# Two more blocks of the residual turned by DMA, and another order of k pairs, in a two-layer trunk kernel

## The chip, the cores and the metric

The kernel runs on one core of one Trainium2 chip. The metric is the device time of one execution in microseconds (us), as the median of several runs. A core has five engines that run side by side, each through its own list of instructions in order: TensorE (PE, matrix products, its weight loads shown as PEld), VectorE (DVE), ScalarE (ACT), GpSimd (POOL) and SyncE (SP), which here issues nearly all DMA transfers. Engines wait for one another through semaphores.

## What is computed

The reference is a decoder trunk of two layers over a residual stream h of 256 rows and 2048 columns, in float32:

```python
for layer in range(DEPTH):                       # DEPTH = 2
    xn = rms_norm(h, norm_mix[layer])
    mix = swa_mlstm_mixer(xn, ...) if layer % 2 == 0 else forgetting_attention_mixer(xn, ...)
    h = h + mix                                  # both mixers end in "@ w_out"
    h = h + swiglu(rms_norm(h, norm_ffn[layer]), w_gate[layer], w_up[layer], w_down[layer])
return rms_norm(h, norm_final)

def swiglu(xn, w_gate, w_up, w_down):            # 2048 -> 5632 -> 2048
    return (silu(xn @ w_gate) * (xn @ w_up)) @ w_down
```

The change lies where a mixer's output projection (`@ w_out`) ends and the gate and up products of the same layer begin.

## The kernel before, in words

Every product is made in three passes: each float32 operand is split into a high part in the fast float32r format and a low part, the remainder, and PE adds high x high, high x low and low x high (lines 192 to 194 and `three`, lines 402 to 404). The activations sit transposed in `xh`/`xl` (after a norm) and `mh`/`ml` (a mixer's heads or the hidden columns), 16 k-tiles of 128. The weights come in chunks of two k-tiles by 512 columns: SP loads a chunk into `raw` (line 105), ACT casts it to `hi` (line 161), DVE subtracts to `lo` (line 162). There are four `raw` buffers (pool `wr`) and six of `hi` and `lo` each (pool `wp`). One chunk feeds 12 matmuls.

`out_proj` (line 386) makes the four blocks n of 512 columns of the mixer's output, two at a time: first 12 of 16 k-tiles of both, then the last four k-tiles of one and of the other. After each block `add_out` (line 300, DVE) adds it to h, and `square_sum` (line 215, ACT) sums its squares for the next norm. Then the block of h has to be transposed into `xh`/`xl`, k-tiles 4n to 4n+3, that is the k pairs 2n and 2n+1. The kernel has two ways:

- `split_scaled` (line 238): PE transposes 128 x 128 pieces into PSUM (line 245), ACT multiplies by the norm's gain to `xh` (line 252), DVE makes `xl` (line 253).
- `split_turned` (line 268): ACT copies the two 16-bit halves of each number into two planes (line 272), SP issues four DMA transposes (line 274); later `join` lets ACT weave the planes together (line 279) and goes on as above from SBUF. It needs two scratch tiles (`scrap`, line 284), which borrow buffers of a later use.

Before the change blocks 0 and 1 are turned by DMA, while the other two blocks are being multiplied; blocks 2 and 3 are turned on PE. `LATER` gives the step of out_proj at which a join is issued; `run_due` (line 172) issues it behind the latest cast of a chunk.

`ffn` (line 473) takes 11 groups of 512 hidden columns, in parts of three, four and four; after each part its down product follows. A group is `pair_group` (line 409): it walks the eight k pairs of `xh` in the order of `ORDER`, for gate and up together. A pair marked 0 is plain: two chunks, 24 matmuls (here called P). A pair marked 1 is taken in seven products in place of eight (here called M): DVE makes four sums and differences of the weights in `t4` (lines 440 to 443), ACT and DVE split them into `ht` and `lt` (lines 294 and 295), and PE makes 21 matmuls against sums of the activations (`sx`), which `sums_of` (line 227) made when the block was split. Four PSUM banks hold the plain sums and four the products; the next group takes them the other way round. `c` and `u2` (lines 466 to 470) put the products together, line 494 adds the plain banks.

The order of the instructions on each engine is laid by the framework's planner from the dependencies; only `run_due` sets a bound by hand. SP's queue holds the loads and the DMA transposes in one order.

Of the kernel before, what the change touches and what calls it, by code (L numbers as in the profile page):

```python
# [7 lines left out]
F32 = mybir.dt.float32  # L8
BF16 = mybir.dt.bfloat16
F32R = mybir.dt.float32r  # L10
# [7 lines left out]
P = 128  # L18
# [3 lines left out]
KT = D // P  # L22
FF = 5632
NB = 512
CK = 2
# [7 lines left out]
OFF_QM, OFF_KM, OFF_VM, OFF_OM = 1536, 2048, 2560, 3584  # L33
CAP = 15.0
FILL = 24
ORDER = ((0, 0), (0, 1), (1, 2), (0, 4), (1, 3), (0, 5), (1, 6), (0, 7))
DOWN = {
    6: ((0, 0), (0, 1), (1, 2), (0, 3), (0, 4), (0, 5)),
    8: ((0, 0), (0, 1), (0, 3), (1, 2), (0, 4), (1, 5), (0, 6), (0, 7)),
}  # L40
MID = 6
MID_DOWN = 5
LATER = (6, 10)
LATER_DOWN = (5, 6)
RAWS = 4
PARTS = (0, 3, 7, 11)
# [2 lines left out]
def mixed_of(order):  # L49
    return [p for w, p in order if w]  # L50
# [5 lines left out]
def trunk(  # L56
# [110 lines left out]
    def new_acc():  # L167
        return [pa.tile([P, NB], F32, tag="acc", name="acc") for _ in range(NT)]

    later = []  # L170
# [6 lines left out]
    def gemm(acc, lhs, w, c0, n, k_from, k_to, k_all, skew=1, step=0):  # L177
        k0 = k_from
        while k0 < k_to:
            last = k_to == k_all and k0 + skew * CK >= k_all  # L180
            chunks = [load_chunk(w, kc, c0, n) for kc in range(k0, k_all if last else k0 + CK, CK)]
            run_due(later, step + k0 // CK)
            order = [(i, t) for i in range(len(chunks) * CK) for t in range(NT)]
            if last:
                order.sort(key=lambda it: it[1])
            for i, t in order:
                k = k0 + i
                hi, lo = (c[:, i % CK, 0:n] for c in chunks[i // CK])
                ah, al = lhs(k)
                ts = slice(t * P, (t + 1) * P)  # L190
                o = acc[t][:, 0:n]
                nc.tensor.matmul(o, ah[:, ts], hi, start=(k == 0), stop=False)  # L192
                nc.tensor.matmul(o, ah[:, ts], lo, start=False, stop=False)  # L193
                nc.tensor.matmul(o, al[:, ts], hi, start=False, stop=(k == k_all - 1))  # L194
            k0 += len(chunks) * CK
# [14 lines left out]
    def square_sum(key, n):  # L210
        if n == 0:
            sums[key] = sm.tile([P, NT, 4], F32, tag="ss", name="ss")
        for t in range(NT):
            junk = sm.tile([P, NB], BF16, tag="junk", name="junk", bufs=1)
            nc.scalar.activation(
                junk, h[:, t, n * NB : (n + 1) * NB], AF.Square, accum_out=sums[key][:, t, n : n + 1]
            )
# [9 lines left out]
    def sums_of(pool, sh, sl, copies, full=None):  # L227
        if full is None:
            full = pool.tile([P, 2, NT, P], F32, tag="tmp", name="full")
            copies(full.rearrange("p i t q -> p i (t q)"))  # L230
        s = pool.tile([P, 4, P], F32, tag="tmp", name="s4")
        nc.vector.tensor_tensor(out=s[:, 0, :], in0=full[:, 0, 1, :], in1=full[:, 1, 1, :], op=ALU.add)
        nc.vector.tensor_tensor(out=s[:, 1, :], in0=s[:, 0, :], in1=full[:, 0, 0, :], op=ALU.subtract)
        nc.vector.tensor_tensor(out=s[:, 2, :], in0=full[:, 0, 0, :], in1=full[:, 0, 1, :], op=ALU.subtract)
        nc.vector.tensor_tensor(out=s[:, 3, :], in0=full[:, 1, 0, :], in1=s[:, 1, :], op=ALU.subtract)
        split_plain(sh, sl, s)

    def split_scaled(idx, n, extra=None, joined=None):
        for half in range(2):
            if joined is None:  # L240
                pt = pm.tile([P, 2, NT, P], F32, tag="pm", name="pt")
                for i in range(2):
                    k = 4 * n + 2 * half + i
                    for t in range(NT):
                        nc.tensor.transpose(pt[:, i, t, :], h[:, t, k * P : (k + 1) * P], ident)  # L245
            else:
                pt = joined[:, 2 * half : 2 * half + 2, :].rearrange("p i (t q) -> p i t q", t=NT)
            for i in range(2):
                k = 4 * n + 2 * half + i
                src = pt[:, i, :, :].rearrange("p t q -> p (t q)")  # L250
                g = gT[:, idx * KT + k : idx * KT + k + 1]
                nc.scalar.mul(xh[:, k, :], src, g)
                nc.vector.scalar_tensor_tensor(
                    out=xl[:, k, :], in0=src, scalar=g, in1=xh[:, k, :].bitcast(F32), op0=ALU.mult, op1=ALU.subtract
                )
            pair = 2 * n + half
            if extra is not None and pair in mixed_of(ORDER):
                sh, sl, pool = extra
                j = mixed_of(ORDER).index(pair)

                def copies(full):
                    for i in range(2):
                        g = gT[:, idx * KT + 2 * pair + i : idx * KT + 2 * pair + i + 1]
                        nc.scalar.mul(full[:, i, :], pt[:, i, :, :].rearrange("p t q -> p (t q)"), g)

                sums_of(pool, sh[:, j, :, :], sl[:, j, :, :], copies)

    def split_turned(idx, n, flat, turned, extra=None):
        planes = flat.bitcast(U16).rearrange("p (b t n) -> p b t n", b=2, t=NT)
        hu = h[:, :, n * NB : (n + 1) * NB].bitcast(U16).rearrange("p t (n b) -> p t n b", b=2)  # L270
        for b in range(2):
            nc.scalar.copy(planes[:, b, :, :], hu[:, :, :, b])
            for t in range(NT):
                nc.sync.dma_start_transpose(turned[:, b, :, t, :], planes[:, b, t, :])

        def join():
            ju = flat.bitcast(U16).rearrange("p (n b) -> p n b", b=2)
            for b in range(2):
                nc.scalar.copy(ju[:, :, b], turned[:, b, :, :, :].rearrange("p k t q -> p (k t q)"))
            split_scaled(idx, n, extra, flat.rearrange("p (k s) -> p k s", k=4))  # L280

        return join

    def scrap(fp, n):
        if n == 0:
            box = fp.tile([P, 4, NB], F32, tag="c", name="box", bufs=1)
            halves = box[:, 0:2, :], box[:, 2:4, :]
        else:
            halves = [fp.tile([P, CK, NB], F32, tag="raw", name="box", bufs=RAWS) for _ in range(2)]
        flat, turned = (a.rearrange("p a n -> p (a n)") for a in halves)  # L290
        return flat, turned.bitcast(U16).rearrange("p (b k t q) -> p b k t q", b=2, t=NT, q=P)
# [92 lines left out]
            split_plain(mh[:, ks, :], ml[:, ks, :], po)  # L384

    def out_proj(w, idx, key, extra):
        last = KT - 4
        for n0 in (0, 2):
            accs = [new_acc() for _ in range(2)]
            for i in range(2):  # L390
                gemm(accs[i], m_of, w, (n0 + i) * NB, NB, 0, last, KT, step=6 * i)
            for i in range(2):
                gemm(accs[i], m_of, w, (n0 + i) * NB, NB, last, KT, KT, step=6)
                add_out(accs[i], n0 + i)
                if n0 == 0:
                    later.append((LATER[i], split_turned(idx, i, *scrap(extra[2], i), extra)))
                else:
                    split_scaled(idx, n0 + i, extra)
                square_sum(key, n0 + i)

    def three(o, ah, al, hi, lo, start, stop):
        nc.tensor.matmul(o, ah, hi, start=start, stop=False)  # L402
# [67 lines left out]
        nc.vector.tensor_tensor(out=c[:, 3, :], in0=prods[1], in1=c[:, 1, :], op=ALU.add)  # L470
        return plain, c

    def ffn(layer, fp, sx, sd, key, idx_next=None, key_next=None, finish=None):
        r = rstd(key)

        def sums_x(pair):
            j = mixed_of(ORDER).index(pair)
            return sx[0][:, j, :, :], sx[1][:, j, :, :]

        for g0, g1 in zip(PARTS, PARTS[1:]):  # L480
            end = g1 == PARTS[-1]
            nk = 4 * (g1 - g0)
            order = DOWN[nk // 2]
            todo = []
            for g in range(g0, g1):
                par = (g1 - 1 - g) % 2
                plain, c = pair_group(
                    fp, par, x_of, sums_x, [(w_gate[layer], g * NB), (w_up[layer], g * NB)], ORDER, todo
                )
                todo = []  # L490
# [54 lines left out]
                todo = [(MID if g < g1 - 1 else MID_DOWN, join)]  # L545
# [20 lines left out]
            for n0 in (0, 2):  # L566
# [9 lines left out]
                todo = []  # L576
# [10 lines left out]
    def close_layer(layer, w_out, idx, key, **rest):  # L587
        with tc.tile_pool(name=f"fp{layer}", bufs=2) as fp:
            nx = len(mixed_of(ORDER))
            nd = max(len(mixed_of(o)) for o in DOWN.values())  # L590
            sx = [fp.tile([P, nx, 4, P], F32R, name=f"sx{i}", bufs=1) for i in range(2)]
            sd = [fp.tile([P, nd, 4, P], F32R, name=f"sd{i}", bufs=1) for i in range(2)]
            out_proj(w_out, idx, key, (*sx, fp))
            ffn(layer, fp, sx, sd, key, **rest)


    acc0 = new_acc()
# [417 lines left out]
```

## Time and profile before

| what | value |
|---|---|
| median of 3 runs | 2132.01 us (2131.75 to 2132.25) |
| the profiled execution | 2131.7 us |
| its span, first to last instruction | 2130.0 us |
| PE busy | 2113.6 us, 9732 instructions |
| DVE busy | 1666.1 us |
| ACT busy | 1256.1 us |
| DMA transposes of h by out_proj (line 274, with the four of one block at the end of the first layer) | 20 |
| PE transposes of h (line 245) | 88 |
| mean granted TensorE clock | 0.998 |

The first layer's out_proj ends and its gate and up products begin near 348 us, the second layer's near 1428 us. Times of the trace count from the span's start. A busy time is a sum over instructions of one engine. Matmuls overlap in PE's pipeline, so the time that one costs is the distance from its start to the next one's, not its own span.

### The profile page before, as it was taken

To read this page: it belongs to the slowest core of one execution; us is meant where nothing else is said; L and a number is where in the kernel's file an instruction comes from. 1 tells how busy PE (TensorE), PEld (TensorE's weight loads), DVE (VectorE), ACT (ScalarE), POOL (GpSimd) and SP (SyncE) were. 2 spreads that over 40 slices of the span, in tenths; PEclk is the share of its full clock that TensorE was granted. 3 is DMA by queue.
4 is the path that set the end of the run, shared out by engine and by line. 5 is a ranking of instruction groups with operands and counts; after the bars stand their busy time and mean duration, and the time that the engine had idled before them with its cause. 6 is when DMAs were issued, how large, how long until landed. Compare 5 with 4: busy or idle time off the path is not lost.

```text
span 2130.0 us, 26773 instructions
## 1 busy us (share of the span) xinstructions
PE 2113.6 (99%) x9732; PEld 1755.0 (82%) x9732; DVE 1666.1 (78%) x2116; ACT 1256.1 (59%) x1584; POOL 39.6 (2%) x61
## 2 busy tenths in 40 slices
PE   8999999999999999999999999999999999999998
PEld 7888888888888888888888888888888888888886
DVE  6665558998899988998755554579998998889984
ACT  6565457765567646666645544576654667556753
POOL 2010000000000000000010000000000000000000
PEclk9999999999999999999999999999999999999999
DMA  8444547665667666766575564675756666656763
GB/s 268 149 150 148 169 150 265 217 208 197 198 207 225 211 207 193 235 206 198 163 235 168 168 178 142 195 247 187 238 188 208 207 208 206 228 189 208 228 200 125
DMA packets 267941, 421.47 MB, mean 198 GB/s; under 512 B 67136, under 2 KB 75424, under 8 KB 267552
## 3 DMA queue, kind: packets, MB, share of 16 engines
q1 hardware_dynamic: 267136, 416.02, 61.5%
q0 software_dynamic: 624, 3.72, 0.5%
q8 instruction: 76, 1.25, 0.2%
q14 instruction: 57, 0.47, 0.1%
q10 hardware_dynamic: 48, 0.02, 0.0%
HBM read 404.48 MB, written 2.11 MB: 191 GB/s over the span
## 4 chain that ended last, share of the span: by engine, by line
PE 98%; ACT 1%; issue 0%; DMA 0%; DVE 0%; DVEq 0%; POOLq 0%; POOL 0%; ACTq 0%
PE acc L402 17%; PE acc L403 17%; PE acc L404 17%; PE acc L192 10%; PE acc L193 10%; PE acc L194 10%; PE prod L402 4%; PE prod L404 4%; PE prod L403 4%; PE p L323 1%; PE ptm L306 1%; PE po L374 1%; PE pt L245 0%; PE pp L366 0%; PE p L316 0%
## 5 line engine op out<-in xcount | busy, mean ns | idle before, releaser
L161 ACT CAST hi<-raw 128x1024 fp32r<-128x1024 f32 (+1 forms) x692 | 705.1, 1033 | 667.3 <-PE acc L404 314.4
L162 DVE TENSOR_TENSOR lo<-raw,hi 128x1024 fp32r<-128x1024 f32 (+1 forms) x692 | 821.5, 1200 | 314.7 <-ACT hi L161 312.9
L403 PE MATMUL acc<-lo,xh 128*128 128x512 f32 x946 | 368.1, 389 | 0.0
L404 PE MATMUL acc<-hi,xl 128*128 128x512 f32 x946 | 367.2, 389 | 0.0
L402 PE MATMUL acc<-hi,xh 128*128 128x512 f32 x946 | 366.5, 389 | 0.0
L192 PE MATMUL acc<-hi,xh 128*128 128x512 f32 (+3 forms) x736 | 276.7, 377 | 0.8 <-ACT hi L161 0.8
L194 PE MATMUL acc<-hi,xl 128*128 128x512 f32 (+3 forms) x736 | 276.8, 377 | 0.0
L193 PE MATMUL acc<-lo,xh 128*128 128x512 f32 (+3 forms) x736 | 276.3, 375 | 0.0
L404 PEld LDWEIGHTS acc<-hi,xl 128*128 128x128 f32 x946 | 177.6, 188 | 36.9
L403 PEld LDWEIGHTS acc<-lo,xh 128*128 128x128 f32 x946 | 177.6, 188 | 36.7
L402 PEld LDWEIGHTS acc<-hi,xh 128*128 128x128 f32 x946 | 177.6, 188 | 36.6
L295 DVE TENSOR_TENSOR lt<-t,ht 128x1024 fp32r<-128x1024 f32 x168 | 199.7, 1217 | 3.6 <-ACT ht L294 3.6
L403 PE MATMUL acc<-lo,mh 128*128 128x512 f32 x514 | 200.2, 389 | 0.0
L402 PE MATMUL acc<-hi,mh 128*128 128x512 f32 x514 | 200.0, 389 | 0.0
L404 PE MATMUL acc<-hi,ml 128*128 128x512 f32 x514 | 198.5, 389 | 0.0
L294 ACT CAST ht<-t 128x1024 fp32r<-128x1024 f32 x168 | 174.8, 1052 | 20.8 <-PE acc L404 12.8
L192 PEld LDWEIGHTS acc<-hi,xh 128*128 128x128 f32 x736 | 139.0, 189 | 25.0 <-ACT hi L161 1.2
L194 PEld LDWEIGHTS acc<-hi,xl 128*128 128x128 f32 x736 | 139.1, 189 | 24.4 <-issue 0.8
L193 PEld LDWEIGHTS acc<-lo,xh 128*128 128x128 f32 x736 | 139.2, 189 | 24.0 <-issue 0.7
L192 PE MATMUL acc<-hi,mh 128*128 128x512 f32 x320 | 125.2, 391 | 1.2 <-ACT mh L294 1.2
L193 PE MATMUL acc<-lo,mh 128*128 128x512 f32 x320 | 125.3, 392 | 0.0
L194 PE MATMUL acc<-hi,ml 128*128 128x512 f32 x320 | 123.9, 390 | 0.0
(311 smaller groups left out, 2779.4 us busy)
## 6 DMA issues: line engine op xcount, KB each, us to landing
raw<-in_w_gate_dram SPq DMA_DIRECT2D x176, 512.0 KB, 4.3
raw<-in_w_up_dram SPq DMA_DIRECT2D x176, 512.0 KB, 4.6
raw<-in_w_down_dram SPq DMA_DIRECT2D x176, 512.0 KB, 4.6
raw<-in_w_in_odd_dram SPq DMA_DIRECT2D x88, 512.0 KB, 3.8
raw<-in_w_in_even_dram SPq DMA_DIRECT2D x64, 512.0 KB, 4.0
raw<-in_w_out_even_dram SPq DMA_DIRECT2D x32, 512.0 KB, 3.6
raw<-in_w_out_odd_dram SPq DMA_DIRECT2D x32, 512.0 KB, 4.2
raw<-in_w_in_odd_dram SPq DMA_DIRECT2D x8, 272.0 KB, 2.9
```

Of the source, the lines that this page charges most:

```text
L161: latest[0] = nc.scalar.copy(hi[:, :, 0:n], raw[:, :, 0:n])
L162: nc.vector.tensor_tensor(out=lo[:, :, 0:n], in0=raw[:, :, 0:n], in1=hi[:, :, 0:n].bitcast(F32), op=ALU.subtract)
L192: nc.tensor.matmul(o, ah[:, ts], hi, start=(k == 0), stop=False)
L193: nc.tensor.matmul(o, ah[:, ts], lo, start=False, stop=False)
L194: nc.tensor.matmul(o, al[:, ts], hi, start=False, stop=(k == k_all - 1))
L294: nc.scalar.copy(dst_h, src)
L295: nc.vector.tensor_tensor(out=dst_l, in0=src, in1=dst_h.bitcast(F32), op=ALU.subtract)
L306: nc.tensor.transpose(pt[:, i, :], s_, ident)
L323: nc.tensor.matmul(p1[:, jj, :], q_of(j, 1), k_of(j), start=True, stop=True)
L402: nc.tensor.matmul(o, ah, hi, start=start, stop=False)
L403: nc.tensor.matmul(o, ah, lo, start=False, stop=False)
L404: nc.tensor.matmul(o, al, hi, start=False, stop=stop)
```

## The change

The order of the k pairs in gate and up becomes natural, and the pairs taken in seven products become 1, 3 and 5 instead of 2, 3 and 6. Blocks 2 and 3 of out_proj's output also go through `split_turned`; their joins are handed from `out_proj` to `ffn`, where the first group issues them at place 3 and place 5 of the pair order. Their scratch tiles borrow the buffer of `c` (block 2, as block 0 does) and those of `sd0` and `sd1` (block 3).

```diff
-ORDER = ((0, 0), (0, 1), (1, 2), (0, 4), (1, 3), (0, 5), (1, 6), (0, 7))
+ORDER = ((0, 0), (1, 1), (0, 2), (1, 3), (0, 4), (1, 5), (0, 6), (0, 7))
...
-LATER = (6, 10)
+LATER = (6, 10, 3, 5)
...
     def scrap(fp, n):
-        if n == 0:
+        if n % 2 == 0:
             box = fp.tile([P, 4, NB], F32, tag="c", name="box", bufs=1)
             halves = box[:, 0:2, :], box[:, 2:4, :]
+        elif n == 3:
+            halves = [fp.tile([P, CK, NB], F32, tag=f"sd{i}", name="box", bufs=1) for i in range(2)]
         else:
...
     def out_proj(w, idx, key, extra):
-        last = KT - 4
+        last, rest = KT - 4, []
...
-                if n0 == 0:
-                    later.append((LATER[i], split_turned(idx, i, *scrap(extra[2], i), extra)))
-                else:
-                    split_scaled(idx, n0 + i, extra)
+                (later if n0 == 0 else rest).append(
+                    (LATER[n0 + i], split_turned(idx, n0 + i, *scrap(extra[2], n0 + i), extra))
+                )
                 square_sum(key, n0 + i)
+        return rest
...
-    def ffn(layer, fp, sx, sd, key, idx_next=None, key_next=None, finish=None):
+    def ffn(layer, fp, sx, sd, key, todo, idx_next=None, key_next=None, finish=None):
...
             order = DOWN[nk // 2]
-            todo = []
...
-            sd = [fp.tile([P, nd, 4, P], F32R, name=f"sd{i}", bufs=1) for i in range(2)]
-            out_proj(w_out, idx, key, (*sx, fp))
-            ffn(layer, fp, sx, sd, key, **rest)
+            todo = out_proj(w_out, idx, key, (*sx, fp))
+            sd = [fp.tile([P, nd, 4, P], F32R, tag=f"sd{i}", name=f"sd{i}", bufs=1) for i in range(2)]
+            ffn(layer, fp, sx, sd, key, todo, **rest)
```

## The prediction

> **What bounds the kernel now.** I read the page first (busy times, chain), then TensorE's waits, then the stretches of each stage.
>
> ```profile
> span 2130.0 us, 26773 instructions
> PE 2113.6 (99%) x9732; PEld 1755.0 (82%) x9732; DVE 1666.1 (78%) x2116; ACT 1256.1 (59%) x1584; POOL 39.6 (2%) x61
> PE 98%; ACT 1%; issue 0%; DMA 0%; DVE 0%; DVEq 0%; POOLq 0%; POOL 0%; ACTq 0%
> PE pg L146 <- DMA gn<-in_norm_mix_dram: 4.2, 1, 4.2
> PE acc L192 <- ACT mh L294: 1.2, 1, 1.2
> PE pt L245 <- DMA h<-in_x_dram: 0.9, 1, 0.9
> PE acc L192 <- ACT hi L161: 0.8, 1, 0.8
> PE pp L366 <- DVE s L358: 0.2, 1, 0.2
> ```
>
> TensorE is the chain, and it hardly waits: all its waits together are 7.3 us. The stretches show that none lie where the change works.
>
> ```profile
> 365.00:705.00 340.00, 340.00 (x1506) 281.63 (x1505) 308.59 (x373) 210.34 (x228) 0.00 (x0) 1.00 0.66 211
> 347.68:360.41 12.73, 12.73 (x66) 10.62 (x65) 12.29 (x25) 9.73 (x21) 1.63 (x1) 1.00 0.58 191
> 1427.03:1439.80 12.77, 12.77 (x65) 10.64 (x64) 9.64 (x19) 8.80 (x18) 0.71 (x1) 1.00 0.48 159
> ```
>
> The columns are the length, then busy time and count of PE, PEld, DVE, ACT and POOL, then granted clock, DMA share and GB/s. PE fills the feed-forward part (first row) and the two places where out_proj ends and gate/up begins (the others), at full clock. So an edit can gain only the time of PE instructions that it removes; anything else can only be hidden or cost.
>
> **What is removed on PE.** Blocks 2 and 3 of h no longer go through PE transposes (line 245): 16 in each of two layers, 32 in all. The page of groups gives a transpose 0.27 us and a matmul 0.39 us, but their spans overlap, so I count from start to start.
>
> ```profile
> 324.79 0.39 PE L193 MATMUL acc<-lo,mh 128*128 128x512 f32 x1
> 347.45 0.39 PE L194 MATMUL acc<-hi,ml 128*128 128x512 f32 x1
> 347.68 0.38 PE L245 MATMUL pt<-ident,h 128*128 128x128 f32 x2
> 349.98 0.82 PE L245 MATMUL pt<-ident,h 128*128 128x128 f32 x6
> 360.41 0.39 PE L402 MATMUL prod<-hi,xh 128*128 128x512 f32 x1
> 1427.04 0.38 PE L245 MATMUL pt<-ident,h 128*128 128x128 f32 x2
> 1439.80 0.39 PE L402 MATMUL acc<-hi,xh 128*128 128x512 f32 x1
> ```
>
> There are 100 matmul intervals from 324.79 to 347.45, so one takes 22.66/100 = 0.2266 us. In the first layer the stretch from 347.68 to 360.41 holds all 16 transposes and two plain pairs of 24 matmuls: 12.73 - 48 x 0.2266 = **1.85 us**. In the second, 1427.04 to 1439.80 holds 16 transposes and again 48 matmuls: 12.76 - 10.88 = **1.88 us**. That is 0.117 us a transpose, with the slower matmul behind each group counted in. The number of products stays: three pairs of eight in seven products before and after, 5 x 24 + 3 x 21 = 183 matmuls a group (41.5 us). Removed: 3.73 us.
>
> **What is added on ACT, SP and DVE.** Per block: two copies into u16 planes, four DMA transposes, two copies back, then the same gain multiply and subtraction.
>
> ```profile
> L274 SPq DMA_TRANSPOSE box<-box x8: 1200/1261/1891, 1381.8 to 1392.3; - x8
> L272 ACT COPY box<-h x4: 1031/1042/1047, 1380.5 to 1386.9; 128x1024 uint16<-128x1024 uint16 x4
> L279 ACT COPY box<-box x4: 1346/1352/1354, 1389.4 to 1401.4; 128x1024 uint16<-128x1024 uint16 x4
> L253 DVE SCALAR_TENSOR_TENSOR xl<-pt,gT,xh x8: 476/482/485, 1428.5 to 1436.3; 128x256 fp32r<-128x256 f32 x8
> ```
>
> ACT gets 4 x 1.04 + 4 x 1.35 = 9.6 us a layer, SP 8 x 1.26 = 10.1 us. DVE gets nothing: the subtraction takes 0.48 us from PSUM, and 1.67 us for four from the box (a row below), and sums are made for three pairs as before. I cost all of it at nothing on the path, because PE's operands are made well ahead:
>
> ```profile
> 368.13 1.06 ACT L161 CAST hi<-raw 128x1024 fp32r<-128x1024 f32 x1 [1.71 <-PE acc L404]
> 373.25 2.36 DVE L162 TENSOR_TENSOR lo<-raw,hi 128x1024 fp32r<-128x1024 f32 x2 [1.10 <-ACT hi L161]
> 320.06 1.05 ACT L161 CAST hi<-raw 128x1024 fp32r<-128x1024 f32 x1 [3.28 <-DMA raw<-in_w_out_even_dram]
> ```
>
> ACT waits for PE to free a split chunk, and DVE waits for ACT: the six split chunks (6 x 12 x 0.2266 = 16.3 us of PE work) are full. The third row is out_proj's own turned blocks 0 and 1: ACT then starved 3.28 us, and PE did not wait. Without that cover, 9.6 us of ACT a layer would show.
>
> **The wait that moves.** PE now reads blocks 2 and 3 behind a longer chain. Its length is in the layers' block 0, from the sums h to the last subtraction:
>
> ```profile
> 302.55 0.69 DVE L300 TENSOR_TENSOR h<-acc,h 128x512 f32<-128x512 f32 x1 [0.21 <-PE acc L194]
> 315.62 1.69 DVE L253 SCALAR_TENSOR_TENSOR xl<-box,gT,xh 128x256 fp32r<-128x256 f32 x4 [1.79 <-ACT xh L252]
> 1378.47 1.28 DVE L300 TENSOR_TENSOR h<-acc,h 128x512 f32<-128x512 f32 x2
> 1394.07 1.67 DVE L253 SCALAR_TENSOR_TENSOR xl<-box,gT,xh 128x256 fp32r<-128x256 f32 x4
> 346.85 0.68 DVE L300 TENSOR_TENSOR h<-acc,h 128x512 f32<-128x512 f32 x1
> 350.52 1.28 DVE L300 TENSOR_TENSOR h<-acc,h 128x512 f32<-128x512 f32 x2
> ```
>
> Block 0 took from 302.55 + 0.69 = 303.24 to 317.31 = 14.1 us in the first layer, and from 1379.75 to 1395.74 = 16.0 us in the second. I take 16. Block 2's sums end at 347.53, so it is ready at 363.5. It is first read in place 4, after P, M, P, M (P plain, M in seven): 347.68 + 90 x 0.2266 = 368.1, 4.6 us to spare. Block 3 ends at 351.80, is ready at 367.8 and read in place 6, 135 matmuls in, at 378.3: 10.5 us to spare. In the second layer block 2's sums are done before its transposes begin at 1427.04, and there is more room.
>
> **The order of pairs.** M now stands at places 1, 3, 5 instead of 2, 4, 6. Its t4, ht and lt have buffers for one M, so it is prepared as soon as the M before it is done. From one M to the next lies one P inside a group and three across the edge, in both orders; only the edge is shifted by one P. Two things come sooner. The first M of a layer starts at 347.68 + 24 x 0.2266 = 353.1, and the first M of a later group takes over the last group's four banks from 5.4 us after the edge.
>
> ```profile
> 339.04 1.22 DVE L295 TENSOR_TENSOR lt<-t,ht 128x1024 fp32r<-128x1024 f32 x1
> 394.00 1.28 DVE L494 TENSOR_TENSOR c<-acc,c 128x512 f32<-128x512 f32 x2
> ```
>
> The first M's lt is done at 340.26, 13 us early. The edge after the first group lies at 347.68 + 1.85 + 41.47 = 391.0; the last bank is freed at 395.28 and wanted 39 matmuls in, at 399.8: 4.5 us to spare. Both cost nothing.
>
> **Sum.** 2132.01 - 3.73 = **2128.3 us** (-0.17%). The profiled execution took 2131.7, 1.7 outside its span of 2130.0; its span would be 2126.3. The median lies 0.3 above that execution, and I take the difference from the median.
>
> **The rivals.** *Part of it is given back in the first layer.* DVE is busy 12.29 of the 12.73 us in which the first layer's transposes stand. PE would reach the second matrix of place 0 at 347.68 + 12 x 0.2266 = 350.4, and its bank is freed by the first of the two sums at 350.52, about 351.2. If DVE keeps that order, 0.8 us are lost; if DVE bounds the whole stretch, 1.85. That gives 2129.1 to 2130.1. Against it: the planner lays DVE's order anew, and line 300's operand was complete 12 matmuls ahead of 347.68, at 345.0, so the sum has 5 us of room.
>
> *Block 2 comes late.* Block 1 of the same layer took longer than block 0, since its join stood behind other work:
>
> ```profile
> 305.27 0.68 DVE L300 TENSOR_TENSOR h<-acc,h 128x512 f32<-128x512 f32 x1
> 331.96 0.48 DVE L253 SCALAR_TENSOR_TENSOR xl<-box,gT,xh 128x256 fp32r<-128x256 f32 x1
> ```
>
> From 305.95 to 332.44 it took 26.5 us. With that, block 2 is ready at 374.0 and PE waits 5.9 us: 2134.2 at most, as in the second layer there is room. Here a join is due at step 10 of out_proj, there at place 3, so most of the 26.5 is waiting for its due step. The Trainium skill speaks for this rival (VectorE: DVE Perf Modes, Rules for kernel authors): turn 128x128 on TensorE where PSUM will do as the destination, by the DMA crossbar otherwise. The trace agrees with it on latency and not on price:
>
> ```profile
> 1428.53 0.48 DVE L253 SCALAR_TENSOR_TENSOR xl<-pt,gT,xh 128x256 fp32r<-128x256 f32 x1 [0.42 <-ACT xh L252]
> ```
>
> From the first PE transpose (1427.04) to the end of the first subtraction are 2.0 us, by DMA 16; but PE is the full engine here, and SP is not.
>
> *Loads stand behind the transposes (slower).* Weight loads and transposes share SP's queue in order, and a transpose waits there for ACT's copy.
>
> ```profile
> 305.11 10.45 SPq L274 DMA_TRANSPOSE box<-box  x8
> SPq L523 <- ACT c L521: 60.2, 20, 9.6
> raw<-in_w_gate_dram SPq DMA_DIRECT2D x176, 512.0 KB, 4.3
> 343.95 1.05 ACT L161 CAST hi<-raw 128x1024 fp32r<-128x1024 f32 x1 [0.28 <-DMA raw<-in_w_up_dram]
> ```
>
> The longest hold is 9.6 (waiting) + 10.45 (a train of eight) + 4.3 (landing) + 2.3 (ACT and DVE) = 26.7 us. Against it stand four raw and six split chunks, 10 x 2.72 = 27.2 us. If the raw chunks are empty, as just ahead (ACT waits for loads up to 343.95), 16.3 us are left and PE loses 10.4: 2138.7 with one layer, 2149 with both. It decides from a hold of 16.3 us with empty raws. Against it: out_proj's own train cost PE nothing.
>
> *More goes.* The planner lays everything anew from here on. If the 1.2 us wait for mh at out_proj's head went too, it would be 2127.1.
>
> That the change does nothing it says is excluded by the diff: no block of a mixer's output is left on line 245.
>
> **How the numbers follow.** Forecast 0.60; part given back 0.14; late block 2 0.07; loads held 0.09; more goes 0.10. A measurement of this kernel can tell about 0.2% (4.26 us) from no change: below 2127.75 is faster, above 2136.27 slower. So faster 0.10 (more goes), slower 0.09 (loads held), same 0.81. The range from 2127.0 to 2132.0 takes in the forecast, what is given back, more, and a late block 2 up to 3.7 us; loads held and the far end of a late block 2 are left out, somewhat over 0.1.
>
> **What would show it.** Line 245 falls from 88 to 56 and PE from 9732 to 9700 instructions; line 274 rises from 20 to 36, ACT's busy time by 19 us; PE's waits after 300 us stay at nothing. The forecast is wrong if PE waits at place 0's second matrix (given back), at place 4 for xh of block 2 (late), or for hi and lo with ACT waiting for raw (loads held); and its step on the order of pairs is wrong if PE waits at the first M of each group.

## The result, and the profile after

The changed kernel took 2127.24 us, median of 17 executions (2126.56 to 2128.05); the kernel before, beside it, 2131.46, median of 17 (2130.54 to 2132.25). The ratio is 0.998, with a 95% interval of 0.9973 to 0.9987: a gain of 4.2 us, 0.2%. The forecast was 2128.3, on a base of 2132.01 that three executions had given; from 2131.46 the same sum gives 2127.7.

The page of the kernel after, the same three lines as of before:

```profile
span 2126.3 us, 26802 instructions
...
PE 2110.2 (99%) x9700; PEld 1751.8 (82%) x9700; DVE 1661.0 (78%) x2116; ACT 1272.4 (60%) x1600; POOL 40.7 (2%) x61
...
PE 98%; ACT 1%; issue 0%; DMA 0%; DVE 0%; SPq 0%; DVEq 0%; POOLq 0%; POOL 0%; ACTq 0%
```

32 PE instructions are gone, and the span is 3.7 us shorter. ACT has 16.3 us more work, PE is still the chain. TensorE's waits after:

```profile
PE pg L146 <- DMA gn<-in_norm_mix_dram: 3.8, 1, 3.8
PE pt L245 <- DMA h<-in_x_dram: 1.4, 1, 1.4
PE acc L192 <- ACT mh L296: 1.2, 1, 1.2
PE acc L192 <- ACT hi L161: 0.8, 1, 0.8
PE pp L368 <- DVE s L360: 0.2, 1, 0.2
```

They are the five of before, at the same places; no new one came. (Lines after 283 stand two lower than before: `add_out` is line 302, `three` 404 to 406.) What moved, from the views of the tiles `pt` and `box`, with durations as minimum, median and maximum in ns:

```profile
L245 PE MATMUL pt<-ident,h x56: 270/273/478, 5.5 to 1042.6; 128*128 128x128 f32 x56
...
L274 SPq DMA_TRANSPOSE box<-box x36: 1188/1260/1894, 305.5 to 1433.0; - x36
```

Line 245 has gone from 88 to 56 and line 274 from 20 to 36. The stretches where out_proj ends and gate and up begin, in the kernel after (length, then busy time and count of PE, PEld, DVE, ACT, POOL, then granted clock, DMA share, GB/s):

```profile
345.00:358.00 13.00, 13.00 (x59) 10.77 (x58) 10.37 (x15) 11.79 (x18) 0.69 (x1) 1.00 0.91 186
...
1424.00:1437.00 13.00, 13.00 (x59) 10.76 (x58) 7.76 (x11) 12.78 (x21) 0.71 (x1) 1.00 0.93 224
```

PE is full, and 59 instructions in 13.00 us are 0.22 us each: matmuls only. ACT is close to full in the second stretch, and PE does not wait for it.

**Where the time went.** Executions of one kernel lie up to 2.1 us apart (2130.13 to 2132.20 in 33 of the kernel before), so a total can't tell a term of 1.8 us from scatter. Inside one trace the distance between two fixed PE instructions can. I take four markers: the third of the four groups of transposes of the mLSTM heads' output (ptv), the first product of the forget gates (pcf), the first product of the last attention group (po), and the last matmul. Before, then after:

```profile
279.83 0.60 PE L841 MATMUL ptv<-ident,hv 128*128 128x128 f32 x4
...
1061.55 0.29 PE L889 MATMUL pcf<-nl,upper 128*128 128x16 f32 x2
...
1355.48 0.60 PE L374 MATMUL po<-t,vn 128*128 128x256 f32 x2
...
2120.54 0.39 PE L194 MATMUL acc<-hi,ml 128*128 128x512 f32 x1
```

```profile
280.20 0.60 PE L842 MATMUL ptv<-ident,hv 128*128 128x128 f32 x4
...
1060.20 0.29 PE L890 MATMUL pcf<-nl,upper 128*128 128x16 f32 x2
...
1354.12 0.60 PE L376 MATMUL po<-t,vn 128*128 128x256 f32 x2
...
2117.26 0.39 PE L194 MATMUL acc<-hi,ml 128*128 128x512 f32 x1
```

From ptv to pcf (the first layer's out_proj and feed-forward part) it took 781.72 us before and 780.00 after; from po to the end (the second layer's) 765.06 and 763.14. Between pcf and po nothing was changed, and the two traces agree there: 293.93 and 293.92. The granted clock shows 1.00 in all stretches from the first marker on, before and after. So the change is worth -1.72 and -1.92, **-3.64 us** in all, against -1.85 and -1.88 in the prediction. The same measure for the experiments that leave these markers in place:

| kernel | first layer | between | second layer | against before |
|---|---|---|---|---|
| before | 781.72 | 293.93 | 765.06 | |
| after | 780.00 | 293.92 | 763.14 | -3.64 |
| order of pairs alone | 781.80 | 293.94 | 765.03 | +0.05 |
| blocks turned, old order | 779.91 | 293.93 | 763.13 | -3.74 |
| block 3 alone turned | 780.90 | 293.93 | 764.08 | -1.80 |
| before, transposes of blocks 2, 3 doubled | 783.52 | 293.96 | 766.79 | +3.53 |
| after, joins one place later | 780.04 | 294.03 | 763.13 | -3.61 |
| after, end of layer 0: block 1 turned too, scratch from raw | 789.61 | 290.76 | 763.14 | +2.80 |
| the same, scratch of its own | 778.96 | 293.93 | 763.13 | -4.69 |

The last column adds the differences of the first and the second layer; in the row with 290.76, where the planner moved work across the marker, that of the stretch between as well.

### The profile page after: what moved, and what is told of

Its sections match the earlier page's. It is cut to its first block, busy times and chain, and to the rows that moved or that the text cites. A ratio compares the mean times of both kernels' runs of the same rounds, so it can differ in the third digit from the quotient of the medians.

```text
span 2126.3 us, 26802 instructions
## 1 busy us (share of the span) xinstructions
PE 2110.2 (99%) x9700; PEld 1751.8 (82%) x9700; DVE 1661.0 (78%) x2116; ACT 1272.4 (60%) x1600; POOL 40.7 (2%) x61
## 4 chain that ended last, share of the span: by engine, by line
PE 98%; ACT 1%; issue 0%; DMA 0%; DVE 0%; SPq 0%; DVEq 0%; POOLq 0%; POOL 0%; ACTq 0%
PE acc L404 17%; PE acc L405 17%; PE acc L406 17%; PE acc L192 10%; PE acc L194 10%; PE acc L193 10%; PE prod L404 4%; PE prod L405 4%; PE prod L406 4%; PE p L325 1%; PE ptm L308 1%; PE po L376 1%; DMA h<-in_x_dram 0%; PE pp L368 0%; PE p L318 0%
```

## The experiments

The theory: the gain is the time, start to start, of the PE transposes removed, and all that came instead is hidden. The rivals: the order of pairs has a part in it; something was given back, and more could have come; the hiding is luck, and the train of transposes in SP's queue costs PE dearly once its cover (the chunks that stand ready for PE while the queue is held) is smaller.

### The order of pairs alone

```diff
-                (later if n0 == 0 else rest).append(
-                    (LATER[n0 + i], split_turned(idx, n0 + i, *scrap(extra[2], n0 + i), extra))
-                )
+                if n0 == 0:
+                    later.append((LATER[i], split_turned(idx, i, *scrap(extra[2], i), extra)))
+                else:
+                    split_scaled(idx, n0 + i, extra)
```

> The natural order of pairs alone; blocks 2 and 3 stay on PE transposes. My theory: the order is worth nothing, since the gain is the PE transposes alone: 0.0 us against the kernel before (within 0.5), and PE waits behind 300 us stay at nothing. Rival (the order brings the gain, because the first M and the edges of groups move): the whole -4 us would show here. Rival (the order costs, and the transposes bring more than 3.7): slower than before by some tenths of a us.

2131.65 against 2131.10 beside it; ratio 1.0002 (0.9993 to 1.0011); stretches +0.05. The medians differ by 0.55 us, inside the interval. Natural order with pairs 1, 3 and 5 in seven products brings nothing and costs nothing: the prediction's step holds.

### Blocks turned, old order

```diff
-ORDER = ((0, 0), (1, 1), (0, 2), (1, 3), (0, 4), (1, 5), (0, 6), (0, 7))
+ORDER = ((0, 0), (0, 1), (1, 2), (0, 4), (1, 3), (0, 5), (1, 6), (0, 7))
...
-LATER = (6, 10, 3, 5)
+LATER = (6, 10, 2, 5)
```

> All four blocks turned, but the old order of pairs, so block 2 is first read at place 3 (pair 4, 69 matmuls = 15.6 us behind the start of gate and up, about 363.7) and its join is due at place 2. My theory: in the changed kernel block 2 was ready at 365.5, 17.4 us behind the start of gate and up, so PE waits up to 2 us in the first layer and perhaps in the second: between -3.7 and 0 us against before, likeliest -2.5. Rival (the order does not matter because the planner moves PE's matmuls between places): -3.7 us, no wait of PE. Rival (the order brings the gain): 0 or slower than before.

2126.93; ratio 0.9981 (0.9972 to 0.999); stretches -3.74, so my -2.5 was wrong. The old order wants block 2 (pair 4) at place 3, sooner than the new one. I had taken the chain's length as fixed. The join, due at place 2, came sooner too; of this kernel, DVE's sum and last subtractions for block 2, then PE's first matmul of that pair, from the timeline (start, us, engine, line):

```profile
346.58 0.68 DVE L302 TENSOR_TENSOR h<-acc,h 128x512 f32<-128x512 f32 x1
...
359.96 1.67 DVE L253 SCALAR_TENSOR_TENSOR xl<-box,gT,xh 128x256 fp32r<-128x256 f32 x4
```

```profile
363.34 0.39 PE L404 MATMUL acc<-hi,xh 128*128 128x512 f32 x1
```

The sums ended at 347.26, so the chain took 14.4 us and block 2 was ready at 361.63, 1.7 us ahead of its reader. Natural order is not needed to hide the transposes either; it adds some room (1.7 us to spare here, 3.0 in the changed kernel, worked out below).

### Block 3 alone

```diff
-                (later if n0 == 0 else rest).append(
-                    (LATER[n0 + i], split_turned(idx, n0 + i, *scrap(extra[2], n0 + i), extra))
-                )
+                if n0 + i == 2:
+                    split_scaled(idx, 2, extra)
+                else:
+                    (later if n0 == 0 else rest).append(
+                        (LATER[n0 + i], split_turned(idx, n0 + i, *scrap(extra[2], n0 + i), extra))
+                    )
```

> The changed kernel with block 2 turned on PE again, so 8 transposes a layer go instead of 16. My theory, 0.117 us a transpose: half the gain, -1.9 us against before (PE instructions 9716). Rival (a fixed cost of switching between transposes and products, paid as soon as any transposes are left): clearly less than half, about -1 us. Rival (it is the eight-long train on SP that matters): not half but all or nothing.

2128.67; ratio 0.9989 (0.9981 to 0.9998); stretches -1.80, half of the whole. Both blocks bring the same, so neither of them waits.

### The transposes doubled in the kernel before

```diff
-                        nc.tensor.transpose(pt[:, i, t, :], h[:, t, k * P : (k + 1) * P], ident)
+                        for _ in range(2 if extra is not None else 1):
+                            nc.tensor.transpose(pt[:, i, t, :], h[:, t, k * P : (k + 1) * P], ident)
```

> The kernel before with each of the 32 PE transposes of blocks 2 and 3 made twice in a row into the same place; the results are the same. My theory: price by itself 0.11 us for a transpose behind another, +3.5 us (3.0 to 3.8) against before. Rival (transposes lie in time in which PE would wait anyway for DVE): less than 1 us. Rival (the spans of 0.27 us on the page add up): +8.7 us.

2134.49; ratio 1.0016 (1.0007 to 1.0025); stretches +3.53. The 32 extra transposes write the same values again and cost 0.110 us each; the 32 removed by the change gave back 3.64/32 = 0.114. The price of a transpose is nearly the same by adding and by taking away, and it is less than half of the 0.27 us that the page of groups shows for one.

### The end of the first layer: block 1 turned as well

At the end of the first feed-forward part, block 0 of h already goes by DMA. This takes block 1 too, 8 more PE transposes; its scratch takes two of the four `raw` buffers.

```diff
-                    if n < 1:
+                    if n < 2:
                         todo.append((LATER_DOWN[n], split_turned(idx_next, n, *scrap(fp, n))))
```

> The changed kernel, and at the end of the first layer's feed-forward part block 1 of h goes by DMA too (as block 0 does there), so 8 more PE transposes go. My theory (each PE transpose costs 0.117 us and a turned block is free while its chain of 14 to 18 us fits ahead of its first use): -4.6 us against before, -0.9 against the changed kernel; in the trace the stretch of the first layer falls by 0.9 us against the changed kernel, the other stretches stay. Rival (the down product at the layer's end has less cover, since its groups hold one or two M and their scratch takes two of the four raw buffers of M): a wait of PE there of 1 us or more, no gain or a loss.

2133.64 against 2131.09 beside it; ratio 1.0012 (1.0003 to 1.0021), slower than before, and about 6.4 us behind the changed kernel in the stretches. SP's queue near the end of the first layer (start, us, instruction, count), then what ACT waited for from 995 to 1066 us (total, times, longest), of this kernel:

```profile
967.77 26.68 SPq L105 DMA_DIRECT2D raw<-in_w_down_dram  x11
994.54 10.47 SPq L274 DMA_TRANSPOSE box<-box  x8
1005.06 12.20 SPq L105 DMA_DIRECT2D raw<-in_w_down_dram  x7
```

```profile
ACT hi L161 <- DMA raw<-in_w_down_dram: 13.1, 2, 9.1
```

Eleven loads were out when the train of eight transposes began, the others stood behind it, and ACT sat idle 9.1 us at one chunk. PE, which does not wait in this stretch in the changed kernel, now waits seven times, 4.3 us in all. Two causes were possible: the train alone, or the two raw buffers that its scratch took, so that fewer chunks stood ready. The next run tells them apart.

### The same with scratch of its own

```diff
+        elif n == 5:
+            halves = [fp.tile([P, 3, NB], F32, tag=f"sx{i}", name="box", bufs=1) for i in range(2)]
...
-                    if n < 1:
-                        todo.append((LATER_DOWN[n], split_turned(idx_next, n, *scrap(fp, n))))
+                    if n < 2:
+                        todo.append((LATER_DOWN[n], split_turned(idx_next, n, *scrap(fp, 5 * n))))
```

> The kernel of the run that turned block 1 at the first layer's end, with one difference: its scratch borrows the two sx tiles, which are free there, instead of two of M's four raw buffers. Its train on SP stays eight long (10.5 us). Theory A (the train holds the loads and that alone starves ACT): PE still waits some us in the second down product, the first layer's stretch and the one behind it together about 5 to 6 us longer than the changed kernel's. Theory B (the missing raw buffers starve it, the train does not): no wait of PE, together 0.9 us shorter than the changed kernel's.

One execution of 2126.82; stretches -1.04 against the changed kernel, that is 0.13 us for each of the 8 transposes, and no new wait of PE. SP's queue of this kernel:

```profile
968.77 30.18 SPq L105 DMA_DIRECT2D raw<-in_w_down_dram  x14
1000.27 10.40 SPq L274 DMA_TRANSPOSE box<-box  x8
1010.76 1.55 SPq L105 DMA_DIRECT2D raw<-in_w_down_dram  x3
```

The train is as long as before (10.40 against 10.47 us), but 14 loads went ahead of it instead of 11. The train alone is hidden: it costs only where the raw buffers are missing as well. What the missing buffers would cost without the train no run shows.

A second version starts block 1's transposes three steps later, which was meant to make two trains of four:

```diff
+                    elif n == 1:
+                        joins = []
+                        todo.insert(0, (3, lambda: joins.append(split_turned(idx_next, 1, *scrap(fp, 5)))))
+                        todo.append((7, lambda: joins[0]()))
```

> The same, and block 1's transposes start at place 3 of the down product instead of at once, so that two trains of four (5.1 us each) leave room for loads between them. Theory A: the wait of PE goes, and the first layer's stretch and the one behind it are together 0.9 us (8 x 0.117) shorter than the changed kernel's: 2126.3 us, or -4.9 against before. Theory B: the same as the run ahead. A late block 1 would show as a wait of PE in the next layer's first product at k-tile 4.

2125.98 (2125.55 to 2126.83) against 2131.46; ratio 0.9975 (0.9966 to 0.9985). Its first-layer stretch is 778.96 us, the same as in the run ahead. But the train was not split; SP's queue of this kernel:

```profile
999.28 10.40 SPq L274 DMA_TRANSPOSE box<-box  x8
```

ACT made block 1's planes right behind its sums as before, and the eight transposes still stand in one train with no load between them. So this run repeats the one ahead with ten executions; what two trains of four would bring is not shown.

### The joins one place later

```diff
-LATER = (6, 10, 3, 5)
+LATER = (6, 10, 4, 6)
```

> The changed kernel with the joins due one place later (4 and 6 instead of 3 and 5), just ahead of their first use. My theory: block 2 comes at about 368 to 369 in the first layer against its first read near 368.4, so PE waits at most 1 us there, and nothing in the second layer: the first layer's stretch 0 to 1 us longer than the changed kernel's, the second's equal. Rival (the due place only orders the planner's list and the planner fills PE with other products of the group): both stretches equal to the changed kernel's within 0.1 us.

One execution of 2126.65; stretches within 0.1 us of the changed kernel, no wait. A due place in `ffn` only sets what the planner may issue from then on; it still laid the work early enough. So this could not make block 2 late, and the price of a late block 2 stays unmeasured.

### Less cover: four split and two raw chunks, with and without the change

```diff
-    wp = ctx.enter_context(tc.tile_pool(name="wp", bufs=6))
-    wr = ctx.enter_context(tc.tile_pool(name="wr", bufs=4))
+    wp = ctx.enter_context(tc.tile_pool(name="wp", bufs=4))
+    wr = ctx.enter_context(tc.tile_pool(name="wr", bufs=2))
...
-        raw = pool.tile([P, CK, NB], F32, tag="raw", name="raw", bufs=4 if pool is wr else RAWS)
+        raw = pool.tile([P, CK, NB], F32, tag="raw", name="raw", bufs=2 if pool is wr else RAWS)
```

Done to the kernel after, then to the kernel before:

> The changed kernel with less ahead of PE: four split chunks and two raw ones instead of six and four, 6 x 2.72 = 16.3 us of PE work instead of 27.2. The hold of SP in the changed kernel is 10.9 (train) + 4.3 (landing) + 2.3 (ACT and DVE) = 17.5 us. Theory of the prediction (it decides when the hold is longer than the cover): PE now waits for hi or lo at the begin of gate and up, 1 to 3 us in each layer, and the gain over the kernel before with the same buffers is lost: the two stretches of the layers together at least 2 us longer, relative to that kernel, than the -3.64 us of the full buffers. Rival (M's own raw buffers and the planner's order cover the hold anyway): the difference stays at -3.6 us, however much both kernels lose elsewhere.

> The control of the run ahead: the kernel before with the same four split and two raw chunks. It may lose time in each group's own transposes and in out_proj's train, in which PE did not wait with full buffers: both theories expect some us, and the same ones in the run ahead; only the difference between the two tells.

2373.85 and 2361.19, one execution each: with less cover the change costs 12.7 us instead of bringing 4. Both kernels starve all over (PE busy 93%), and the planner laid other parts anew, so the totals mix several things; at the two places of the change the waits can be read one by one. PE's waits there, in the first and in the second layer, of the kernel after with less cover; then what ACT waited for and SP's queue in the first layer; then PE's waits of the kernel before with less cover, first and second layer:

```profile
PE acc L404 <- ACT hi L161: 7.6, 1, 7.6
PE acc L405 <- DVE lo L162: 1.3, 1, 1.3
...
PE acc L404 <- ACT hi L161: 8.1, 1, 8.1
```

```profile
ACT hi L161 <- DMA raw<-in_w_up_dram: 8.3, 1, 8.3
```

```profile
389.88 10.37 SPq L274 DMA_TRANSPOSE box<-box  x8
400.36 0.53 SPq L105 DMA_DIRECT2D raw<-in_w_up_dram  x1
```

```profile
PE acc L402 <- ACT hi L161: 0.8, 1, 0.8
...
PE acc L402 <- ACT hi L161: 0.9, 1, 0.9
```

The train holds the next w_up load for 10.37 us, ACT waits 8.3 us for it, and PE stands 8.9 us (7.6 + 1.3) where it stood 0.8; in the second layer it is 9.4 (8.1 + 1.3) against 0.9. That is the mechanism of the prediction's slower rival, at both places, and it cost far more than the 1 to 3 us a layer that I expected. I had set the 16.3 us of six full chunks against a hold of 17.5, but the chunks were not full. PE in the first layer, where the wait ends:

```profile
405.31 1.22 PE L404 MATMUL acc<-hi,xh 128*128 128x512 f32 x2 [7.63 <-ACT hi L161]
```

From the train's start at 389.88 to this product are 15.4 us, and PE ran out of operands at 405.31 - 7.63 = 397.68, after 7.8 us. So what counts is what stands ready when the train starts; the number of buffers is only its upper bound. In the changed kernel, with its ten chunks, that was enough.

## Why the prediction held, step by step

**PE transposes, -3.73.** Measured -3.64. Doubling them (+3.53) and taking half of them away (-1.80) give the same price from the other side. The term was right in mechanism and size. The totals differ by 4.2, with an interval of 2.8 to 5.8 us (from the ratio) that holds 3.64; the rest is scatter of the executions, a part of which has a cause below. So it is luck of the base and of scatter that the median, 2127.24, came out below the 2127.75 to which the prediction gave a chance of 0.10.

**ACT, SP, DVE at nothing.** ACT's busy time rose by 16.3 us, not 19.2. Two copies in a row overlap (1.98 us for two planes, not 2.08; 2.54 for two weavings, not 2.70, in the rows below), which makes some 1 us of the difference; the rest, and why DVE's fell by 5.1, was not followed up. None of it shows in PE's waits. The cover that I named does the hiding, as the run with less cover shows.

**The chain of block 2, 16 us.** It was 17.6 in the first layer. From the timelines of DVE, ACT and SP of the kernel after, in order of time:

```profile
346.55 1.27 DVE L302 TENSOR_TENSOR h<-acc,h 128x512 f32<-128x512 f32 x2
```

```profile
347.89 1.98 ACT L272 COPY box<-h 128x1024 uint16<-128x1024 uint16 x2
...
356.89 2.54 ACT L279 COPY box<-box 128x1024 uint16<-128x1024 uint16 x2
```

```profile
348.95 10.89 SPq L274 DMA_TRANSPOSE box<-box  x8
359.94 0.53 SPq L105 DMA_DIRECT2D raw<-in_w_gate_dram  x1
```

```profile
363.79 1.67 DVE L253 SCALAR_TENSOR_TENSOR xl<-box,gT,xh 128x256 fp32r<-128x256 f32 x4
...
372.61 1.66 DVE L253 SCALAR_TENSOR_TENSOR xl<-box,gT,xh 128x256 fp32r<-128x256 f32 x4
```

From the sums' end at 347.82 to 365.46 are 17.6 us. The planes are made at once, the four transposes of block 2 are issued in half of the 10.89 us, and the join waits behind ACT's casts. PE reaches place 4 at 348.05 + 90 x 0.2266 = 368.4: 3.0 us to spare, where I had 4.6. Block 3 is ready at 374.3 and read 45 matmuls later, at 378.6. Block 2 did not come late.

**Part given back.** It did not happen. The planner took products of the first M ahead of the plain pair, which I had not foreseen. PE after, at the edge:

```profile
347.82 0.39 PE L194 MATMUL acc<-hi,ml 128*128 128x512 f32 x1
348.05 0.39 PE L404 MATMUL prod<-hi,xh 128*128 128x512 f32 x1
348.28 0.39 PE L404 MATMUL prod<-ht,sx 128*128 128x512 f32 x1
```

The products go into other banks (`prod`) than those that the last block of out_proj holds, so PE had work while DVE made its sums. The move was not needed: with the old order PE went on with the plain pair at once, and lost nothing either (-3.74). No wait of PE for these sums shows in either trace, which fits the prediction's other reason, that they have room.

**Loads held.** The mechanism is real, and its deciding quantity was the right one: the chunks that stand ready against the time that the train holds the queue. In the kernel as it is ACT never waits for raw between 345 and 380 us. These are all its waits there:

```profile
ACT hi L161 <- PE acc L194: 2.1, 1, 2.1
ACT junk L215 <- DVE h L302: 0.6, 1, 0.6
```

The rival's bound of 10.4 us was made for empty raw buffers, which this kernel did not meet; the 8.9 us with less cover lie near it, but come from another hold (15.4 us, not 26.7) and another cover (7.8 us, not 16.3).

**More goes.** The wait for mh is still 1.2 us. What is below the forecast is the base, 0.55 us, and scatter.

Not shown: what a late block 2 would cost, and what the change would give if ACT were as full as PE.

## What to carry to other kernels

Price an instruction of the full engine from start to start amid its neighbours, not by its span: 0.27 us on the page were 0.11 us of time. Work moved to a queue that also carries the loads is free as long as the chunks ready at that moment last until the first load behind the train has landed and been split (15.4 us with less cover, where 7.8 us stood ready). Count them at that place, and beware of paying for scratch with the load buffers that are the cover: here that turned a gain of 1.0 us into a loss of 6.4. Measure small terms between two fixed instructions of one trace, where they repeated here to 0.1 us, when whole executions scatter by 1 us.

## What had not been expected: a dip of the clock behind small products

The scatter has a cause that is no part of the change. In the first layer's mixer eight products have 4 rows of operand (line 750 before, 751 after). Behind them the granted clock (third column from the end) falls, in the kernel before and after:

```profile
189.00:192.00 3.00, 3.00 (x13) 2.26 (x13) 2.25 (x7) 2.59 (x9) 0.00 (x0) 0.75 0.13 48
192.00:195.00 3.00, 3.00 (x13) 2.39 (x13) 1.82 (x2) 0.90 (x1) 0.00 (x0) 0.68 0.00 0
```

```profile
189.00:192.00 3.00, 3.00 (x14) 2.32 (x13) 2.62 (x7) 2.23 (x8) 0.00 (x0) 0.82 0.28 107
192.00:195.00 3.00, 3.00 (x11) 2.37 (x11) 1.70 (x2) 1.27 (x3) 0.00 (x0) 0.61 0.00 0
```

There a matmul takes 0.43 us from start to start instead of 0.2266. It does not come in every execution: those with a mean clock of 0.999 are faster than those with 0.998, in the changed kernel 6 with a median of 2126.67 against 11 with 2127.59. In six traces with the dip, ptv comes at 279.6 to 280.2 us; in the five without it at 278.2 to 278.8, some 1.2 us sooner (the first experiment below has the dip and 278.9, and the two kernels with less cover aren't counted).

A first try moved the products to another place in the text, behind the first gate projection:

```diff
         with tc.tile_pool(name="mp", bufs=1) as mp:
+            gate_out(project(wi, OFF_OM, NB), 0, NB)
             dt_ = mp.tile([P, ML_H, NT, P], F32, name="dt_")
...
-            gate_out(project(wi, OFF_OM, NB), 0, NB)
```

> Nothing of the change: the changed kernel with the eight products of four rows (pb) and the exponentials behind them moved behind the first of the two gate projections. In some executions the granted clock falls to 0.6 to 0.8 for some 6 us right behind these products (189 to 195 us), in others it does not, and the time differs by about 1 us. Theory (the crowd of small products there, some 9 us of them, brings the dip): spread among large ones, no execution has it, all show 0.999 and the median falls by 0.5 to 1 us against the changed kernel, -4.8 against before. Rival (the dip comes from elsewhere and only shows here): as many executions with 0.998 as before, -4.2.

2127.20; ratio 0.998 (0.9971 to 0.9989). The planner laid them six matmuls earlier instead (186.47 against 187.81 us), the dip is in its trace, and 9 of 11 executions have the lower clock; it tells nothing.

The second try, on top of the second version of own scratch above, gives the products 128 rows, of which 124 are zeros:

```diff
-        mt = ev.tile([4, S], F32, name="mt")
+        mtp = ev.tile([P, S], F32, name="mt")
+        nc.gpsimd.memset(mtp, 0.0)
+        mt = mtp[0:4, :]
...
-        sel = ev.tile([4, ML_H, P], F32, name="sel")
+        sel = ev.tile([P, ML_H, P], F32, name="sel")
...
-                        pb[:, i, :, :].rearrange("p c q -> p (c q)"), sel[:, 2 * g + i, :], mt, start=True, stop=True
+                        pb[:, i, :, :].rearrange("p c q -> p (c q)"), sel[:, 2 * g + i, :], mtp, start=True, stop=True
```

> The fastest kernel so far (own scratch, split train), and the eight products of four rows (pb) made as products of 128 rows, the other 124 filled with zeros; the result is the same. Theory (products that use few of TensorE's rows bring the clock dip behind them): no execution has the dip, all show 0.999, the median falls by 0.3 us to about 2125.7. Rival (the dip does not hang on the rows in use): about six executions in ten with 0.998, median 2126.0 as without the padding.

The products in the changed kernel and here (the form is rows x columns of the operands), then the stretches here:

```profile
187.81 1.97 PE L751 MATMUL pb<-mt,sel 4*128 4x256 f32 x8
```

```profile
187.48 1.99 PE L761 MATMUL pb<-mt,sel 128*128 128x256 f32 x8
```

```profile
189.00:192.00 3.00, 3.00 (x20) 2.51 (x18) 2.59 (x8) 2.62 (x7) 0.00 (x0) 1.00 0.21 81
192.00:195.00 3.00, 3.00 (x17) 2.47 (x16) 2.25 (x3) 1.57 (x4) 0.00 (x0) 1.00 0.27 39
```

They take the same time with 128 rows as with 4, 7 of 7 executions have the clock of 0.999, and the time is 2124.66 us (2124.39 to 2125.99) against 2131.30; ratio 0.9969 (0.9958 to 0.9981). This is the fastest kernel of the study. Without the padding 5 of 10 executions had the lower clock (median 2126.71) and 5 had not (2125.72), so 7 of 7 by chance would be 1 in 128. This run was on another chip, but the kernel before, beside it there, had the lower clock in 10 of 11. So the 4 rows of these products are a likely cause, not a shown one: one kernel alone speaks for it, the planner also laid the products 0.45 us earlier than without it, and the still smaller products of 4 rows just ahead of them (`pn`) were left as they are. That the padded kernel also lies 1.1 us below the undisturbed five is not explained; its stretches from ptv on are the same within 0.05 us, and ptv comes 0.56 us earlier.
